# A hybrid recurrence and attention layer on one core: the attention's reciprocal and normalising product move from VectorE to GpSimd

## The chip, the core and the metric

The program runs on one core of a Trainium2 chip. The core has five engines with a queue each: TensorE (PE, with its weight loads shown apart as PEld), VectorE (DVE), ScalarE (ACT), GpSimd (POOL) and SyncE (SP, which issues most transfers). Each engine takes its instructions strictly in the order of its own queue, and an instruction that waits holds up everything behind it. The metric is the device time of one execution in microseconds (us); lower is better.

## The reference, cut to what matters

Two layers run over 256 context tokens and 256 grid tokens, 1024 wide. Each layer projects the tokens to 4096 columns, runs a gated linear recurrence (4 heads) and a neighbourhood attention (8 heads of 64) side by side, projects the two back, and ends in a mixture of 16 experts of which two are used per token. In the second layer only the grid tokens are asked for. The attention's softmax is what the change touches:

```python
s_lat = jnp.where(mask, s_lat + bias.astype(f32), MASK_VALUE)
s_ctx = jnp.einsum('bhrqd,bhkd->bhrqk', grid(q_plain), k_ctx).astype(f32) * scale
p = jax.nn.softmax(jnp.concatenate([s_lat, s_ctx], axis=-1), axis=-1).astype(v.dtype)
...
o = (jnp.einsum('bhrqk,bhrkd->bhrqd', p[..., :n_lat], v_blk)
     + jnp.einsum('bhrqk,bhkd->bhrqd', p[..., n_lat:], v_ctx))
```

## The kernel before, in words

The part of a layer before the output projection is called the front here (`front`, L471). It walks over 16 chunks of 256 projected columns. For each chunk a weight block comes from HBM, ACT makes its rounded high part `wh` (L422), DVE or POOL the remainder `wl` (L423, called a split below), and PE runs three products per pair of tiles (L427 to L429). The table `SPL` says which engine makes which of a chunk's four splits. Only four `wh` and four `wl` buffers exist, one chunk's worth.

As soon as their columns are there, two kinds of other work are put between the chunks: a recurrence head (`hgrn`, L696, whose long chain runs mostly on DVE, with its rms power at L824 on POOL) and a pair of attention heads (`attention`, L868). Four such pairs run in each layer. A pair is a row of units, one for each 128 query tokens and each of the two heads: 8 units in the first layer (four with 256 keys, four with 512), 4 units with 512 keys in the second. That makes 48 units, 16 of 256 columns and 32 of 512.

One unit is a chain over all engines: PE makes the scores `ats` (L881, L882), DVE adds the bias if the keys are grid tokens (L886) and finds the negated row maximum (L888), ACT takes the exponential `ex` and, in a second instruction, delivers its row sum into `sm` (L890), DVE takes the reciprocal of the sum (L891) and multiplies `ex` by it (L892). PE then transposes `ex` by 128 columns at a time into `atp` (L902), ACT copies that out to `pT` (L904), and PE multiplies by the values into `ato` (L913). `units` below are numbered 0 to 47 in the order of time.

Scores and transposes share two PSUM banks (tag "s"), `ex` has three buffers, `sm` four. In the code the scores of unit i+1 stand before the transposes of unit i. The final order on each engine is not the code's: it is set when the program is built, by a scheduler that spreads projection matmuls between the attention's ones. So a changed cost on one engine moves instructions on others too. On POOL the neighbours of a unit's instructions are splits (L423), the clearing of `kl` (L858), the rotary products (L836), the gate products (L647) and the recurrence's K (L713).

Of the kernel before, what the change touches and what calls it, by code (L numbers as in the profile page):

```python
# [13 lines left out]
ALU = mybir.AluOpType  # L14
# [4 lines left out]
P = 128  # L19
# [167 lines left out]
class Emit:  # L187
# [75 lines left out]
    def run(self):  # L263
        tc, nc, A, ctx = self.tc, self.nc, self.A, self.ctx
        pool = lambda *a, **k: ctx.enter_context(tc.tile_pool(*a, **k))
        self.l = 0
        self.cp = pool(name="const", bufs=1)
        self.xp = pool(name="xp", bufs=1)
        self.dp = pool(name="dram", bufs=1, space=DRAM)
        self.mp = pool(name="misc", bufs=1)  # L270
        self.wp = pool(name="wp", bufs=NWP)
        c = lambda shape, name, dt=F32: self.cp.tile(shape, dt, name=name)
        V, G, S = nc.vector, nc.gpsimd, nc.scalar
        self.ct = c([P, NKEEP], "ct")
        self.lb = c([P, 2, 2, 4], "lb")
        self.ln = c([P, 2, 4, KT], "ln")
        self.wr = c([P, KT, NE], "wr")
        self.br = c([P, NE], "br")
        self.bada = c([P, 2, 96], "bada")
        self.ang = c([P, 2, P], "angt")  # L280
        self.ada = [c([P, 48, 2], f"ada{l}") for l in range(2)]
        self.x = [self.xtile(h) for h in range(2)]

        cc = self.mt([P, 512], "lnss", 1)[:, :4 * KT].rearrange("p (i k v) -> p i k v", i=2, v=2)
        q = nc.sync
        q.dma_start(cc[:, 0], A["cT"])
        self.todo = [(l, b, None) for l in range(2) for b in range(24)]
        self.todo[0] = (0, 0, self.wload(A["wada"][0, 0], 2)[:])
        q.dma_start(self.bada[:], A["bada"].rearrange("l p c -> p l c"))
        ne = _C["ident"][1]  # L290
        q.dma_start(self.ct[:, :ne], A["const"][:, :ne])
        S.activation(cc[:, 1], cc[:, 0], AF.Tanh, scale=0.5)
        V.scalar_tensor_tensor(cc[:, 1], cc[:, 1], 1.0, cc[:, 0], op0=ALU.add, op1=ALU.mult)
        self.scw = c([P, KT, 32 + 2 * NADA - 2], "scw")
        G.memset(self.scw[:], 0.0)
        V.tensor_scalar(self.scw[:, :, 2 * NADA - 2:2 * NADA], cc[:, 1], 0.5, None, op0=ALU.mult)

        for o in (8, 32):
            V.tensor_scalar(self.bada[:, :, 2 * o:2 * o + 16], self.bada[:, :, 2 * o:2 * o + 16], 1.0, None, op0=ALU.add)
        for o in (16, 40):  # L300
            V.tensor_scalar(self.bada[:, :, 2 * o:2 * o + 16], self.bada[:, :, 2 * o:2 * o + 16], IA, None, op0=ALU.mult)
        self.ident = self.cst("ident")
        self.tri16 = c([P, P], "tri16", F16)
        self.one16 = c([P, P], "one16", F16)
        self.iota16 = c([P, CAP], "iota16", F16)
        self.ones32, self.e31 = c([P, 32], "ones32"), c([P, 32], "e31")
        self.neghalf = c([P, 8], "neghalf")
        self.ga, self.gna, self.gc = (c([P, 2, 4], n) for n in ("ga", "gna", "gc"))
        self.lt = c([P, 5, 2, 4], "lt")
        self.hD = self.dp.tile([NT, D], F32, name="hD")  # L310
        self.yD = [self.dp.tile([2 * n, D], F32, name=f"yD{i}") for i, n in enumerate((NT, SEQ))]
        self.late = self.open_step = None
        for l in range(2):
            self.l = l
            self.layer(l)
            if self.stop and self.stop.startswith(f"L{l}"):
                return


    def late_constants(self):  # L320
        nc, A, V, G, S = self.nc, self.A, self.nc.vector, self.nc.gpsimd, self.nc.scalar
        q = nc.sync
        ne = _C["ident"][1]
        q.dma_start(self.ct[:, ne:], A["const"][:, ne:NKEEP])
        ints = self.mt([P, 256], "adasb", 4)
        q.dma_start(ints[:, :P + CAP], A["const"][:, NKEEP:NKEEP + P + CAP])
        q.dma_start(self.lb[:], A["lb"])
        q.dma_start(self.ln[:], A["ln"])
        q.dma_start(self.wr[:], A["wr"])
        q.dma_start(self.br[:], A["br"])  # L330
        q.dma_start(self.ang[:], A["ang"].rearrange("l p c -> p l c"))
        for t, i in ((self.ones32, 0), (self.e31, 31)):
            G.memset(t[:], 0.0)
            G.memset(t[:, i:i + 1], 1.0 / D)
        G.memset(self.neghalf[:], -0.5)
        z = self.mt([P, 512], "lnss", 1)
        G.memset(z[:], 0.0)
        self.zero = z[:]

        V.tensor_copy(self.tri16[:], ints[:, :P])  # L340
        G.memset(self.one16[:], 1.0)
        V.tensor_copy(self.iota16[:], ints[:, P:P + CAP])

        lt = self.lt
        l0, l1 = self.lb[:, 0], self.lb[:, 1]
        V.tensor_tensor(lt[:, 0], l0, l1, op=ALU.max)
        V.tensor_tensor(lt[:, 1], l0, lt[:, 0], op=ALU.subtract)
        V.tensor_tensor(lt[:, 2], l1, lt[:, 0], op=ALU.subtract)
        S.activation(lt[:, 1], lt[:, 1], AF.Exp)
        S.activation(lt[:, 2], lt[:, 2], AF.Exp)  # L350
        V.tensor_tensor(lt[:, 3], lt[:, 1], lt[:, 2], op=ALU.add)
        V.reciprocal(lt[:, 3], lt[:, 3])
        V.tensor_tensor(lt[:, 1], lt[:, 1], lt[:, 3], op=ALU.mult)
        V.tensor_tensor(lt[:, 2], lt[:, 2], lt[:, 3], op=ALU.mult)
        V.tensor_tensor(lt[:, 4], lt[:, 1], lt[:, 2], op=ALU.add)
        V.tensor_tensor(lt[:, 4], lt[:, 4], lt[:, 1], op=ALU.subtract)

        V.tensor_scalar(self.ga[:], lt[:, 4], -0.5, 0.5, op0=ALU.mult, op1=ALU.add)
        V.tensor_scalar(self.gna[:], lt[:, 4], 0.5, -0.5, op0=ALU.mult, op1=ALU.add)
        V.tensor_scalar(self.gc[:], lt[:, 4], 0.5, 0.5, op0=ALU.mult, op1=ALU.add)  # L360
# [507 lines left out]
    def attention(self, j, q, k, kl):  # L868
        nc, V, S = self.nc, self.nc.vector, self.nc.scalar
# [5 lines left out]
        def scores(tt, hh):  # L875
            ps = self.pq("s", "ats")
            N = 512 if tt >= 2 else 256
            plain = (slice(N - 256, N), slice(SEQ + 128 * tt - t0, SEQ + 128 * tt - t0 + 128), slice(SEQ, SEQ + CTX))
            rotated = (slice(0, 256), slice(128 * tt - CTX, 128 * tt - CTX + 128), slice(0, SEQ))
            for o, qs, ks in (plain, rotated)[:N // 256]:  # L880
                nc.tensor.matmul(ps[:, o], q[hh][:, qs], k[hh][:, ks], start=True, stop=False, skip_group_check=True)  # L881
                nc.tensor.matmul(ps[:, o], q[hh][:, qs], kl[hh][:, ks], start=False, stop=True, skip_group_check=True)  # L882
            if tt >= 2:
                bt = self.et([P, 256], "bt", NBT)
                S.dma_start(bt[:], self.A["bias"][l, 2 * j + hh, :, tt - 2, :])
                V.tensor_tensor(ps[:, 0:256], ps[:, 0:256], bt[:], op=ALU.add)  # L886
            st = self.mp.tile([P, 4], F32, tag="sm", bufs=4, name="sm")
            V.tensor_reduce(st[:, 0:1], ps[:, :N], axis=AX.X, op=ALU.max, negate=True)  # L888
            e = ex[tt, hh] = self.t2("ex", "e", N)
            S.activation(e[:], ps[:, :N], AF.Exp, bias=st[:, 0:1], accum_out=st[:, 1:2])  # L890
            V.reciprocal(st[:, 2:3], st[:, 1:2])  # L891
            V.tensor_scalar(e[:], e[:], st[:, 2:3], None, op0=ALU.mult)  # L892

        def trans(tt, hh):
            N = 512 if tt >= 2 else 256
# [22 lines left out]
        for i in range(len(units) + 1):  # L918
            if i < len(units):
                scores(*units[i])  # L920
            if i:
                trans(*units[i - 1])
                if units[i - 1][0] % 2 and units[i - 1][1]:
                    values(units[i - 1][0] // 2)
# [839 lines left out]
```

## Time and profile before

| | |
|---|---|
| time before, median of 3 runs | 1307.35 us (1300.77 to 1309.37) |
| the profiled execution | 1303.5 us, of which 1301.7 us from the first to the last instruction (the span) |
| PE busy in the span | 1179.9 us (91%) |
| DVE busy | 591.0 us (45%) |
| ACT busy | 413.6 us (32%) |
| POOL busy | 333.9 us (26%) |
| granted TensorE clock, mean | 0.963 of full speed |

The attention units lie between 168 and 348 us (first layer) and between 876 and 996 us (second). Busy shares over the span hide that: read the stages. A busy PE is an engine with a matmul under way, and matmuls overlap in the records, so that an idle time of PE is the more reliable thing to read. "Idle before" is attributed to the event that ended the wait.

### The profile page before, as it was taken

The page shows a single profiled execution, that of the slowest core. Times are in us where ns is not written, and L with a number is a line of the kernel's source. Part 1 is how long each engine was busy: PE and PEld are TensorE (multiplying, and loading weights), DVE is VectorE, ACT ScalarE, POOL GpSimd, SP SyncE. Part 2 cuts the span into 40 slices and gives each one's busy share as a digit, 9 for nine tenths or more (in the row PEclk, how much of TensorE's full clock was granted, in tenths as well). Part 3 has the DMA queues.
Part 4 walks back from the last instruction along what each step waited for, and adds up shares of the span by engine and source line. Part 5 has one row for each costly group of instructions (what it writes and reads, how often), then busy time and mean ns, then how long its engine had stood idle before and what let it go on. Part 6 is the DMA issues. An engine that isn't in the chain of part 4 may idle for free. (4 is left out here: it accounts for less than half of the span.)

```text
span 1301.7 us, 22530 instructions
## 1 busy us (share of the span) xinstructions
PE 1179.9 (91%) x8821; PEld 731.9 (56%) x8821; DVE 591.0 (45%) x1364; ACT 413.6 (32%) x905; POOL 333.9 (26%) x349
## 2 busy tenths in 40 slices
PE   6989999999898699998997899998888899999984
PEld 4778767668697333333332488976677644333321
DVE  2466654786645414211110764446786434221215
ACT  2233354453544113211111663245436402001011
POOL 2124243322333210111000344254434211112101
PEclk9999999999998699999998899999999989999997
DMA  8794315413275699999997733354235889999994
GB/s 299 251 305 186 145 55 208 142 50 106 90 310 208 262 381 372 392 392 389 408 416 283 271 112 130 130 199 185 105 107 221 369 329 388 390 407 409 423 422 177
DMA packets 67683, 339.30 MB, mean 261 GB/s; under 512 B 10003, under 2 KB 17907, under 8 KB 31856
## 3 DMA queue, kind: packets, MB, share of 16 engines
q1 hardware_dynamic: 54016, 315.73, 62.5%
q0 software_dynamic: 5936, 12.58, 2.9%
q10 hardware_dynamic: 7616, 9.44, 2.3%
q8 instruction: 73, 1.20, 0.4%
q14 instruction: 42, 0.34, 0.1%
HBM read 322.79 MB, written 20.45 MB: 264 GB/s over the span
## 5 line engine op out<-in xcount | busy, mean ns | idle before, releaser
L423 POOL TENSOR_TENSOR wl<-w,wh 128x512 fp32r<-128x512 f32 x121 | 167.0, 1396 | 184.8 <-ACT wh L422 167.1
L1364 PE MATMUL pgA<-we,xgT 128*64 128x512 f32 x688 | 164.6, 612 | 2.6 <-DMA we<-in_wgu_dram 2.6
L427 PE MATMUL pscm<-xh,wh 128*128 128x512 f32 (+1 forms) x320 | 118.2, 374 | 3.5 <-ACT wh L422 2.3
L428 PE MATMUL pscm<-xl,wh 128*128 128x512 f32 (+1 forms) x320 | 119.9, 377 | 0.3 <-DVE xl L423 0.2
L429 PE MATMUL pscm<-xh,wl 128*128 128x512 f32 (+1 forms) x320 | 117.4, 370 | 1.4 <-POOL wl L423 1.4
L422 ACT ACTIVATE wh<-w 128x512 fp32r<-128x512 f32 x160 | 96.6, 626 | 50.6 <-PE pscm L428 17.4
L1364 PEld LDWEIGHTS pgA<-we,xgT 128*64 128x64 f32 x688 | 48.2, 140 | 94.5 <-issue 84.5
L428 PE MATMUL pstm<-wl,xh 128*128 128x256 f32 x320 | 92.4, 289 | 4.5 <-DVE wl L423 3.2
L429 PE MATMUL pstm<-wh,xl 128*128 128x256 f32 x320 | 91.4, 286 | 0.0
L427 PE MATMUL pstm<-wh,xh 128*128 128x256 f32 x320 | 91.0, 285 | 0.0
L1428 POOL DMA_INDIRECT yD<-y,ss x25 | 23.1, 922 | 236.5 <-DVE y L1416 81.6
L1401 PE MATMUL pdA<-we,hdT 128*64 128x512 f32 x320 | 76.4, 611 | 3.3 <-DMA we<-in_wd_dram 3.2
L1364 PE MATMUL pgA<-mw,xgT 128*64 128x512 f32 x336 | 77.7, 598 | 0.0
L1355 DVE COPY xgT<-ptx 128x256 f32<-128x256 f32 (+1 forms) x32 | 15.4, 482 | 135.6 <-PE ptx L1349 90.9
L427 PEld LDWEIGHTS pscm<-xh,wh 128*128 128x128 f32 x320 | 60.6, 191 | 14.3 <-ACT wh L422 2.4
L428 PEld LDWEIGHTS pscm<-xl,wh 128*128 128x128 f32 x320 | 61.3, 192 | 10.5 <-DVE xl L423 0.9
L429 PEld LDWEIGHTS pscm<-xh,wl 128*128 128x128 f32 x320 | 60.8, 191 | 10.7 <-POOL wl L423 2.1
L1382 DVE SCALAR_TENSOR_TENSOR hid<-hid,pgA 128x256 f32<-128x256 f32 x32 | 13.5, 421 | 114.1 <-ACT hid L1381 113.9
L428 PEld LDWEIGHTS pstm<-wl,xh 128*128 128x128 f32 x320 | 61.0, 191 | 6.7 <-DVE wl L423 3.6
L1381 ACT ACTIVATE hid<-pgA 128x256 f32<-128x256 f32 x32 | 12.3, 384 | 160.6 <-PE pgA L1364 160.6
L429 PEld LDWEIGHTS pstm<-wh,xl 128*128 128x128 f32 x320 | 61.1, 191 | 1.0 <-issue 0.8
L427 PEld LDWEIGHTS pstm<-wh,xh 128*128 128x128 f32 x320 | 61.0, 191 | 0.5
(383 smaller groups left out, 2327.3 us busy)
## 6 DMA issues: line engine op xcount, KB each, us to landing
we<-in_wgu_dram SPq DMA_DIRECT2D x86, 1024.0 KB, 14.0
mw<-in_wgu_dram SPq DMA_DIRECT2D x42, 1024.0 KB, 11.1
w<-in_wada_dram SPq DMA_DIRECT2D x41, 1024.0 KB, 7.0
we<-in_wd_dram SPq DMA_DIRECT2D x40, 1024.0 KB, 16.1
w<-in_win_dram SPq DMA_DIRECT2D x29, 1024.0 KB, 5.4
mw<-in_wd_dram SPq DMA_DIRECT2D x24, 1024.0 KB, 16.2
w<-in_wout_dram SPq DMA_DIRECT2D x11, 1024.0 KB, 4.9
wa<-in_wada_dram SPq DMA_DIRECT2D x6, 1024.0 KB, 9.3
```

The source lines that it names most:

```text
L422: self.nc.scalar.activation(hi, src, AF.Copy)
L423: leng.tensor_tensor(lo, src, hi.bitcast(F32), op=ALU.subtract)
L427: mm(out, lh, rh, start=first, stop=False, **k)
L428: mm(out, lh, rl, start=False, stop=False, **k)
L429: mm(out, ll, rh, start=False, stop=last, **k)
L1355: V.tensor_copy(t[:, 0:4, :c], src)
L1364: mm(pA[64 * j:64 * j + 64, :], xgT[e][:, k, 0:64], wk[:, 512 * j:512 * j + 512], start=(k == 0), stop=(k == KT - 1), skip_group_check=Tru ...
L1381: S.activation(h, ps[:, :n], AF.Tanh, scale=0.5)
L1382: V.scalar_tensor_tensor(h, h, 1.0, ps[:, :n], op0=ALU.add, op1=ALU.mult)
L1401: mm(dA[64 * j:64 * j + 64, :], hdT[e][:, kb, 0:64], wk[:, 512 * j:512 * j + 512], start=(kb == 0), stop=(kb == 3), skip_group_check=True, ...
L1428: G.indirect_dma_start(out=self.yD[l][:], out_offset=bass.IndirectOffsetOnAxis(ap=idx, axis=0), in_=y[:c], in_offset=None, bounds_check=2 ...
```

## The change

Two instructions of each unit go from DVE's queue to POOL's. POOL is not given a reciprocal; it raises the sum to the power -1 with a constant tile of -1.0, made once. The product keeps its form, with a scalar for each partition.

```diff
         self.neghalf = c([P, 8], "neghalf")
+        self.negone = c([P, 8], "negone")
...
         G.memset(self.neghalf[:], -0.5)
+        G.memset(self.negone[:], -1.0)
...
             S.activation(e[:], ps[:, :N], AF.Exp, bias=st[:, 0:1], accum_out=st[:, 1:2])
-            V.reciprocal(st[:, 2:3], st[:, 1:2])
-            V.tensor_scalar(e[:], e[:], st[:, 2:3], None, op0=ALU.mult)
+            G = self.nc.gpsimd
+            G.tensor_tensor(st[:, 2:3], st[:, 1:2], self.negone[:, 0:1], op=ALU.pow)
+            G.tensor_scalar(e[:], e[:], st[:, 2:3], None, op0=ALU.mult)
```

In the changed kernel the power is line 894 and the product line 895; lines of the attention behind them stand three further on (the transposes are L905), earlier ones two (the splits are L425).

On POOL, at the start of the first attention pair of the first layer (`wl` are the splits, `kl` the cleared key parts, `K2` the recurrence's K), before:

```order
L423 TENSOR_TENSOR wl_0_1752<-w8_21_1741,wh_0_1751 128x512
L423 TENSOR_TENSOR wl_0_1756<-w8_21_1741,wh_0_1755 128x512
L858 MEMSET kl0_0_1927 64x512
L713 TENSOR_SCALAR K2_0_2332<-uff_1784 128x512
L423 TENSOR_TENSOR wl_0_1844<-w8_24_1841,wh_0_1843 128x512
L423 TENSOR_TENSOR wl_0_1848<-w8_24_1841,wh_0_1847 128x512
L858 MEMSET kl1_0_1928 64x512
```

and in the change:

```order
L425 TENSOR_TENSOR wl_0_1754<-w8_21_1743,wh_0_1753 128x512
L425 TENSOR_TENSOR wl_0_1758<-w8_21_1743,wh_0_1757 128x512
L894 TENSOR_TENSOR sm_1598<-sm_1598,negone_102 128x1
L895 TENSOR_SCALAR ex_1600<-ex_1600,sm_1598 128x256
L894 TENSOR_TENSOR sm_1607<-sm_1607,negone_102 128x1
L895 TENSOR_SCALAR ex_1609<-ex_1609,sm_1607 128x256
```

The first unit's power stands behind all four splits of the chunk that PE is about to use; on POOL nothing stood there before.

On POOL, in the second half of the same pair (units 5 to 7), before:

```order
L858 MEMSET kl0_0_1927 64x512
L713 TENSOR_SCALAR K2_0_2332<-uff_1784 128x512
L423 TENSOR_TENSOR wl_0_1844<-w8_24_1841,wh_0_1843 128x512
L423 TENSOR_TENSOR wl_0_1848<-w8_24_1841,wh_0_1847 128x512
L858 MEMSET kl1_0_1928 64x512
L423 TENSOR_TENSOR wl_0_1852<-w8_24_1841,wh_0_1851 128x512
```

and in the change:

```order
L894 TENSOR_TENSOR sm_1675<-sm_1675,negone_102 128x1
L860 MEMSET kl0_0_1929 64x512
L895 TENSOR_SCALAR ex_1677<-ex_1677,sm_1675 128x512
L715 TENSOR_SCALAR K2_0_2334<-uff_1786 128x512
L425 TENSOR_TENSOR wl_0_1846<-w8_24_1843,wh_0_1845 128x512
L894 TENSOR_TENSOR sm_1696<-sm_1696,negone_102 128x1
L895 TENSOR_SCALAR ex_1698<-ex_1698,sm_1696 128x512
L860 MEMSET kl1_0_1930 64x512
L425 TENSOR_TENSOR wl_0_1850<-w8_24_1843,wh_0_1849 128x512
L894 TENSOR_TENSOR sm_1716<-sm_1716,negone_102 128x1
L895 TENSOR_SCALAR ex_1718<-ex_1718,sm_1716 128x512
L425 TENSOR_TENSOR wl_0_1854<-w8_24_1843,wh_0_1853 128x512
```

Each of the last two units now has one split ahead of its power, and the last splits of the next chunk stand behind the units' powers and products.

On PE, units 2 and 3 of that pair (`ats` scores, `atp` transposes, `pscm` projection), before:

```order
L881 MATMUL ats_1629<-ks1_0_1425,qs1_0_1384 128x256
L882 MATMUL ats_1629<-kl1_0_1427,qs1_0_1384 128x256
L428 MATMUL pscm_1759<-xl4_0_130,wh_0_1751 128x512
L902 MATMUL atp_1638<-ct_69,ex_1621 128x128 x2
L429 MATMUL pscm_1759<-xh4_0_122,wl_0_1752 128x512
L427 MATMUL pscm_1759<-xh5_0_123,wh_0_1751 128x512
L428 MATMUL pscm_1759<-xl5_0_131,wh_0_1751 128x512
L881 MATMUL ats_1642<-ks0_0_1424,qs0_0_1383 128x256
```

and in the change:

```order
L883 MATMUL ats_1631<-ks1_0_1427,qs1_0_1386 128x256
L884 MATMUL ats_1631<-kl1_0_1429,qs1_0_1386 128x256
L905 MATMUL atp_1640<-ct_69,ex_1623 128x128 x2
L430 MATMUL pscm_1761<-xl4_0_131,wh_0_1753 128x512
L431 MATMUL pscm_1761<-xh4_0_123,wl_0_1754 128x512
L429 MATMUL pscm_1761<-xh5_0_124,wh_0_1753 128x512
L883 MATMUL ats_1644<-ks0_0_1426,qs0_0_1385 128x256
```

One projection matmul that stood ahead of the transposes now stands behind them.

## Rows read from the trace of the kernel before

**Rows 1.** The page: busy us and share of the span, each engine.
```profile
PE 1179.9 (91%) x8821; PEld 731.9 (56%) x8821; DVE 591.0 (45%) x1364; ACT 413.6 (32%) x905; POOL 333.9 (26%) x349
```

**Rows 2.** Windows around attention pairs: length, busy by engine, clock, DMA; sum over eight.
```profile
165.00:190.00 25.00, 22.32 (x126) 16.28 (x124) 14.56 (x30) 13.68 (x34) 10.82 (x10) 1.00 0.20 64
875.00:891.00 16.00, 10.94 (x64) 8.41 (x62) 15.59 (x35) 10.05 (x24) 8.29 (x8) 1.00 0.57 221
...
sum 159.00, PE 141.40 PEld 108.56 DVE 111.50 ACT 92.97 POOL 51.31; mean PE 17.67 PEld 13.57 DVE 13.94 ACT 11.62 POOL 6.41
```

**Rows 3.** Line 902, the transposes: what ended PE's waits, us and times.
```profile
  DVE ex L892: 9.6, 11
  DVE sm L891: 2.7, 2
```

**Rows 4.** PE's other waits, 150 to 400 and 740 to 1010: total us, times, longest.
```profile
PE hgt L662 <- DVE ah L659: 3.2, 2, 1.7
...
PE hgX L776 <- DVE K L797: 4.0, 2, 2.9
```

**Rows 5.** DVE by line and form: busy us, mean ns, idle before.
```profile
L892 DVE TENSOR_SCALAR ex<-ex,sm 128x512 f32<-128x512 f32 x32 | 17.1, 535 | 0.7
...
L891 DVE RECIPROCAL sm<-sm 128x1 f32<-128x1 f32 x48 | 7.6, 158 | 12.8 <-ACT ex L890 12.7
L892 DVE TENSOR_SCALAR ex<-ex,sm 128x256 f32<-128x256 f32 x16 | 6.8, 428 | 0.4
```

**Rows 6.** Single lines: shortest, median, longest ns, first and last start, form.
```profile
L892 DVE TENSOR_SCALAR ex<-ex,sm x48: 342/479/1491, 169.2 to 994.1; 128x512 f32<-128x512 f32 x32, 128x256 f32<-128x256 f32 x16
L1660 POOL TENSOR_TENSOR lnst<-lnst,neghalf x2: 577/1048/1520, 1291.9 to 1294.0; 128x1 f32<-128x1 f32 x2
L1078 POOL TENSOR_TENSOR lnst<-lnst,neghalf x5: 697/702/726, 389.7 to 1031.5; 128x2 f32<-128x2 f32 x5
L713 POOL TENSOR_SCALAR K<-uff x4: 621/693/802, 63.9 to 220.4; 128x512 f32<-128x512 f32 x4
```

**Rows 7.** Timeline of unit 0: start us, us, instruction, idle before.
```profile
167.24 3.83 POOL L423 TENSOR_TENSOR wl<-w,wh 128x512 fp32r<-128x512 f32 x3
168.34 0.39 PE L427 MATMUL pscm<-xh,wh 128*128 128x512 f32 x1
168.57 0.40 PE L428 MATMUL pscm<-xl,wh 128*128 128x512 f32 x1
168.75 0.20 ACT L890 ACTIVATION_READ_ACCUMULATOR ex<-ats,sm 128x1 f32 x1
168.99 0.16 DVE L891 RECIPROCAL sm<-sm 128x1 f32<-128x1 f32 x1 [0.62 <-ACT ex L890]
169.18 0.75 DVE L892 TENSOR_SCALAR ex<-ex,sm 128x256 f32<-128x256 f32 x1
170.08 0.41 PE L902 MATMUL atp<-ct,ex 128*128 128x128 f32 x2 [0.41 <-DVE sm L891]
```

**Rows 8.** Timeline of unit 6.
```profile
182.30 0.19 ACT L890 ACTIVATION_READ_ACCUMULATOR ex<-ats,sm 128x1 f32 x1
...
183.53 1.84 DVE L712 TENSOR_SCALAR F<-F 128x512 f32<-128x512 f32 x1
185.47 0.49 DVE L892 TENSOR_SCALAR ex<-ex,sm 128x512 f32<-128x512 f32 x1
186.10 0.63 PE L902 MATMUL atp<-ct,ex 128*128 128x128 f32 x4 [2.10 <-DVE ex L892]
```

**Rows 9.** Timeline of unit 45.
```profile
987.73 0.19 ACT L890 ACTIVATION_READ_ACCUMULATOR ex<-ats,sm 128x1 f32 x1
989.17 0.65 PE L902 MATMUL atp<-ct,ex 128*128 128x128 f32 x4
```

**Rows 10.** Timeline near the end: the longer power of line 1660, and DVE beside it.
```profile
1294.03 1.52 POOL L1660 TENSOR_TENSOR lnst<-lnst,neghalf 128x1 f32<-128x1 f32 x1 [1.60 <-DVE lnst L1659]
...
1293.86 1.27 DVE L1662 SCALAR_TENSOR_TENSOR zt<-zt,lnst,ln 128x1024 f32<-128x1024 f32 x1
```

## The prediction, made before the change was run

> **What bounds the kernel now.** The page's first part gives PE 91% of the span and POOL 26% [rows 1]. That invites the thought that POOL has room for anything, but an average over 1302 us says nothing about the stretches where the attention runs, so I read windows next. Around the eight attention pairs (159 us together) PE is busy 141.4 us, DVE 111.5 and POOL 51.3 [rows 2]. PE still sets the pace there, and it idles 17.6 us. One of these windows is different: from 875 to 891 us DVE is busy 15.59 of 16.00 us and PE only 10.94. There DVE sets the pace.
>
> Then the wait itself. PE waits 9.6 us for the product and 2.7 us more, 13 times in all, at the transposes [rows 3]. These 12.3 us are the most that a faster product chain could give back at this place. Elsewhere PE's largest waits on DVE are in the recurrence, 4.0 and 3.2 us [rows 4]. So nothing near the whole busy time of the two moved instructions is to be had, and what counts is the length of one chain: from the row sum (end of the accumulator read) to the first transpose.
>
> **The price of one unit.** On an unhindered DVE a unit takes 0.04 us to start, 0.16 for the reciprocal, 0.04 for the step between them and then the product, 0.34 for 256 columns or 0.48 for 512 [rows 6, 7]: 0.58 or 0.72 us. On POOL I price it so. The power: the trace has the same operation for one column twice, at 0.58 and 1.52 us, and for two columns five times, close to 0.70 [rows 6]. I take 0.70, the row that repeats; the ends of the range are 0.58 and the mean of the first two, 1.05. The product: POOL's one-input form of 512 columns takes 0.62 at best and 0.69 in the middle [rows 6]; I take 0.68. For 256 columns no row exists; between half of that (0.34) and all of it (0.68), I take 0.42, nearer to half. Starting costs 0.04 as on DVE, and for the step between the two, 0.06, an estimate. That makes 1.22 us for 256 columns and 1.48 for 512, against 0.58 and 0.72. Every unit's chain is twice as long if both engines are free.
>
> **Where it lies on the path.** DVE was often not free. Unit 0 shows the cheap case: sum at 168.95, transposes at 170.08, because the product ran 0.75 us beside splits on POOL [rows 7]. The new chain would let PE start at 168.95 + 1.22 + 0.15 = 170.32, 0.24 later (0.15 us is what passes in every unit between a product's end and its transposes). Unit 6 shows the other: its sum is there at 182.49, but DVE is inside a 1.84 us instruction of the recurrence, the product ends at 185.96 and PE has waited 2.10 us [rows 8]. POOL would be ready for PE at 184.12, 1.98 earlier. Done so for all 48 units, one after the other in the timeline, 27 come later by 10.2 us together (the first is unit 0, the last unit 45, which goes from 989.17 to 989.55 [rows 7, 9]), and 21 come earlier or had slack; counting of those only what PE's waits hold, they give 7.8 us. Net: +2.4 us.
>
> **POOL's queue.** The order of the change puts unit 0's power behind all four splits. The last of them ends at 171.07 [rows 7], 2.1 us after the sum, so unit 0 starts its power there and PE its transposes at 172.40 (with 0.70 + 0.06 + 0.42 + 0.15) instead of 170.32: +2.1 us more. In later units too a split stands ahead of a power, as at the second place shown above; at three of the 48 (units 14, 15 and 44) POOL reaches that split late. Half a split of 3.83/3 = 1.28 us each: +1.9 us. The splits that now stand behind powers come later by one to three microseconds; PE waited for almost none of them before, and I price this at 1 us, between nothing and three.
>
> **Moved matmuls.** The scheduler puts transposes ahead of one projection matmul in about ten units, as shown for unit 2. Matmuls start 0.23 us apart [rows 7]. Where PE then waits for POOL anyway, that filler has lost its use: 10 times 0.23, half of it counted, +1.1 us.
>
> **What DVE gives back.** 7.6 + 17.1 + 6.8 = 31.5 us of DVE's busy time go [rows 5]. DVE is not the pace in seven of eight windows, so most of that hides beside PE. It helps where PE waits for the recurrence: of the 7.2 us [rows 4] I count 40%, -3 us. The one memset that makes the constant stands in an early stretch where POOL idles: nothing. Exponentials, copies and values stay as they are, and no transfer is added. On SP's queue one expert block of the second layer moves behind ten others of its kind; the same bytes go in the same stretch, so I cost it nothing, at worst the few us of one block. What the fronts lose or win reaches the end of the kernel: behind each front PE has the same work, and in the second layer the expert loads on SP's queue wait for buffers that the last attention pair frees.
>
> **The sum:** 2.4 + 2.1 + 1.9 + 1.0 + 1.1 - 3.0 = +5.5 us, against the profiled execution of 1303.5 us: 1309.0. That execution lies 3.85 us below the median of the runs, 1307.35, so for the median I predict 1307.35 + 5.5 = 1312.9, rounded to **1313 us**. A change of 1%, 13 us, is about what a measurement of this kernel tells from none; this is within it.
>
> **Rival 1, slower: POOL's power costs what its worse row says.** The 1.52 us power at 1294.03 began while a DVE instruction with two SBUF inputs (1.27 us from 1293.86) was running and ended after it; the 0.58 us one did not have that [rows 6, 10]. In the attention windows DVE is busy 111.5 of 159 us [rows 2], much of it with such instructions, so many powers could meet one. Place: all 48 units. At 1.05 us on average the same reading of the timeline gives 35 units that come later by 20.8 us and waits given back of only 5.2: +15.6 in place of +2.4. In the first pair POOL's 10.82 busy us of 25 [rows 2] would become 10.82 + 8 x 1.05 + 4 x 0.42 + 4 x 0.68 = 23.6, so its queue would be the pace there. It decides from a mean of about 0.9 us upwards. Time: 1307.35 + 5.5 + 13.2 = 1326. Against it: the five two-column powers hardly vary. Chance 0.22.
>
> The Trainium skill (SBUF — State Buffer, "Who interferes with whom") says that GpSimd and VectorE share a pair of SBUF ports as an exclusive lock, and that a VectorE instruction with two SBUF inputs excludes a GpSimd one that reads SBUF, whichever began second waiting for the whole of the other. By that rule 1.05 or more would be the price wherever the recurrence runs beside a unit, and the time 1326. The trace agrees with the rule in the one case of 1.52 us, and the 0.75 us product beside splits is the same from the other side; how often a power meets such an instruction no row shows.
>
> **Rival 2, faster: the waits on DVE vanish.** If most of the longer chains are covered by projection matmuls, what remains is that DVE no longer stands in PE's way: the 12.3 us at the transposes [rows 3] and half of the 7.2 in the recurrence [rows 4] go, and of the 10.2 us of later starts half is hidden. 1307.35 - 12.3 - 3.6 + 5.1 = 1297. For it speaks the window from 875 us, where DVE is full. Against it: the scheduler put the transposes nearer to the scores, not farther, so cover was taken away. Chance 0.12, half of it past 1%.
>
> **Chances and range.** My forecast, 1304 to 1320, has 0.66; rival 1 has 0.22, rival 2 0.12. Faster by over 1% (below 1294.3): half of rival 2, 0.06. Slower by over 1% (above 1320.4): rival 1, 0.22. The rest, 0.72, is within 1%. The range runs from 1299, which cuts off the better part of rival 2, to 1329, which takes in rival 1 with the upper price of the power.
>
> **What the changed profile would show.** The power (L894) near 0.7 us and the product (L895) near 0.42 and 0.68: the price holds; a mean power of 0.9 or more is rival 1. PE's wait at the transposes (L905), now on POOL, between 14 and 20 us where 12.3 were; under 8 is rival 2. In the window of the second layer's first pair (around 875 us) DVE should have 2 to 3 us less and PE idle less; in the first pair PE should wait some 2 us more at the first transposes, behind the splits. POOL's busy time should grow by 48 x 0.70 + 32 x 0.68 + 16 x 0.42 = 62 us, DVE's fall by 31. I would be wrong if the new order moved something outside the fronts: the expert part behind each front should keep its length.

## The result, and the profile after

| | before | after |
|---|---|---|
| median of the runs, us | 1304.06 (1297.36 to 1309.37) | 1350.67 (1348.54 to 1356.37) |
| the profiled execution: time, span, us | 1303.5, 1301.7 | 1352.3, 1350.4 |
| PE busy / not busy in the span, us | 1179.9 / 121.8 | 1194.5 / 155.9 |
| granted clock, mean | 0.963 | 0.952 |

The change makes the kernel slower: 1.0359 times the time of before, 95% interval 1.0331 to 1.0387. That is 47 us where 5.5 were forecast, and it lies above the whole range (1299 to 1329).

First the page's busy line of the changed kernel, which answers [rows 1].

```profile
PE 1194.5 (88%) x8821; PEld 740.6 (55%) x8821; DVE 564.6 (42%) x1268; ACT 414.4 (31%) x905; POOL 425.9 (32%) x446
```

DVE lost 26.4 us, as the 31.5 of [rows 5] said roughly. POOL gained 92 us where 62 were forecast: the moved instructions cost more than they were priced at. PE runs the same 8821 matmuls and is busy 14.6 us longer, since it had the lower clock for more of the time. The other 34.1 of the span's 48.7 us are idle time of PE. Nearly all of the loss lies where the attention runs: from the first row sum to the last transposes the first layer takes 32.0 us longer (210.9 for 179.0) and the second 14.1 (132.3 for 118.2).

The second view takes POOL's instructions by line and form (busy us, mean ns, idle before), as [rows 5] did for DVE:

```profile
L895 POOL TENSOR_SCALAR ex<-ex,sm 128x512 f32<-128x512 f32 x32 | 51.5, 1609 | 3.1
L894 POOL TENSOR_TENSOR sm<-sm,negone 128x1 f32<-128x1 f32 x48 | 27.9, 581 | 41.6 <-ACT ex L892 41.3
...
L895 POOL TENSOR_SCALAR ex<-ex,sm 128x256 f32<-128x256 f32 x16 | 15.5, 970 | 1.6
```

The power (L894) is cheaper than the 0.70 us forecast. The product (L895) takes 1.61 and 0.97 us, over twice the 0.68 and 0.42 of the forecast. The single lines (shortest, median, longest ns), to hold against [rows 6]:

```profile
L894 POOL TENSOR_TENSOR sm<-sm,negone x48: 537/567/1017, 167.9 to 1038.3; 128x1 f32<-128x1 f32 x48
...
L895 POOL TENSOR_SCALAR ex<-ex,sm x48: 925/1569/2064, 168.5 to 1039.2; 128x512 f32<-128x512 f32 x32, 128x256 f32<-128x256 f32 x16
```

The median power lies 0.03 us above the shortest one, so at most a few had to wait for something else (the mean is 0.58). The slow product is no tail either: its median is at 1.57.

The page's row for the transposes shows what PE paid (busy us, mean ns, idle before):

```profile
L905 PE MATMUL atp<-ct,ex 128*128 128x128 f32 x160 | 30.7, 311 | 49.0 <-POOL ex L895 48.8
```

49.0 us of waiting stand where the two lines of [rows 3] made 12.3. The waits of PE in the two attention parts, first 150 to 420 us, then 770 to 1060 (total us, times, longest):

```profile
PE atp L905 <- POOL ex L895: 31.6, 25, 3.8
...
PE hgt L664 <- DVE ah L661: 1.4, 1, 1.4
...
PE atp L905 <- POOL ex L895: 17.1, 11, 4.5
PE hgX L778 <- DVE K L799: 4.0, 2, 2.9
...
PE hgt L664 <- DVE ah L661: 0.9, 1, 0.9
```

PE's waits for `ah`, 3.2 us in the first part [rows 4], are down to 1.4, and in the second from 2.6 to 0.9; the wait for `K` is the 4.0 us it was. So DVE's relief is worth 3.5 us here, and no more.

The timeline of unit 0, to hold against [rows 7] (start us, us, instruction, idle before):

```profile
164.14 3.75 POOL L425 TENSOR_TENSOR wl<-w,wh 128x512 fp32r<-128x512 f32 x3
...
165.66 0.20 ACT L892 ACTIVATION_READ_ACCUMULATOR ex<-ats,sm 128x1 f32 x1
...
167.87 0.55 POOL L894 TENSOR_TENSOR sm<-sm,negone 128x1 f32<-128x1 f32 x1
...
168.51 0.94 POOL L895 TENSOR_SCALAR ex<-ex,sm 128x256 f32<-128x256 f32 x1
169.42 0.56 POOL L894 TENSOR_TENSOR sm<-sm,negone 128x1 f32<-128x1 f32 x1
...
169.50 0.69 PE L905 MATMUL atp<-ct,ex 128*128 128x128 f32 x2 [2.96 <-POOL ex L895]
...
170.42 0.63 PE L431 MATMUL pscm<-xh,wl 128*128 128x512 f32 x1
```

The sum is there at 165.86. The power stands behind the splits until 167.87, the product runs to 169.45, and PE has waited 2.96 us. Then a second cost is to be seen: the two transposes take 0.69 us where they took 0.41 [rows 7], and a projection matmul 0.63 instead of 0.39. From 169.2 to 172.6 us the records have the granted clock at half (1.2 instead of 2.4 GHz), after PE had stood idle.

I take one measure from the records of single instructions for all that follows: the time from the row sum (end of the accumulator read) to the end of the product, summed over the 48 units, called **the chains**. Before they make 62.6 us: 19.5 until the reciprocal starts, 7.6 of it, 11.5 until the product starts and 24.0 of that. After they make 136.2 us: 33.6, 27.9, 7.7 and 67.0.

### The profile page after: what moved, and what is told of

The parts are those of the page before. It is cut to its first block, busy times and chain, and to the rows that moved or that the text cites. A ratio compares the mean times of both kernels' runs of the same rounds, so it can differ in the third digit from the quotient of the medians.

```text
span 1350.4 us, 22562 instructions
## 1 busy us (share of the span) xinstructions
PE 1194.5 (88%) x8821; PEld 740.6 (55%) x8821; DVE 564.6 (42%) x1268; ACT 414.4 (31%) x905; POOL 425.9 (32%) x446
## 5 line engine op out<-in xcount | busy, mean ns | idle before, releaser
L425 POOL TENSOR_TENSOR wl<-w,wh 128x512 fp32r<-128x512 f32 x121 | 165.8, 1386 | 168.9 <-ACT wh L424 141.3
L905 PE MATMUL atp<-ct,ex 128*128 128x128 f32 x160 | 30.7, 311 | 49.0 <-POOL ex L895 48.8
L895 POOL TENSOR_SCALAR ex<-ex,sm 128x512 f32<-128x512 f32 (+1 forms) x48 | 67.0, 1396 | 4.7
L1384 ACT ACTIVATE hid<-pgA 128x256 f32<-128x256 f32 x32 | 12.3, 383 | 162.8 <-PE pgA L1367 162.8
## 6 DMA issues: line engine op xcount, KB each, us to landing
we<-in_wgu_dram SPq DMA_DIRECT2D x86, 1024.0 KB, 15.8
mw<-in_wd_dram SPq DMA_DIRECT2D x24, 1024.0 KB, 17.3
wa<-in_wada_dram SPq DMA_DIRECT2D x6, 1024.0 KB, 12.3
```

What stands on the lines that cost most here:

```text
L425: leng.tensor_tensor(lo, src, hi.bitcast(F32), op=ALU.subtract)
L895: G.tensor_scalar(e[:], e[:], st[:, 2:3], None, op0=ALU.mult)
L905: nc.tensor.transpose(pt[:, 128 * n:128 * n + 128], ex[tt, hh][:, 128 * n:128 * n + 128], self.ident)
L1384: S.activation(h, ps[:, :n], AF.Tanh, scale=0.5)
```

## The experiments

All ratios are to the kernel before, run on the same chip. The theories were: **price** (the two instructions are longer on POOL than forecast), **queue** (POOL gets to them late), **clock** (PE's lower clock makes the loss by itself), and rival 1 of the prediction (the power waits for DVE).

### One of the two instructions alone

The product alone on POOL, the reciprocal on DVE:

```diff
             V.reciprocal(st[:, 2:3], st[:, 1:2])
-            V.tensor_scalar(e[:], e[:], st[:, 2:3], None, op0=ALU.mult)
+            G.tensor_scalar(e[:], e[:], st[:, 2:3], None, op0=ALU.mult)
```

> Reciprocal on DVE again, only the product on POOL. Theory (the product's own duration on POOL, 1.57 us for 512 columns and 0.93 for 256, is what the time went to): the chain from sum to product end is 0.04 + 0.16 + 0.1 + 1.57 = 1.9 us instead of 2.3, so about 0.4 us x 48 units of at most half exposed are given back: 10 us below the change, ratio to before about 1.027. Rival (POOL's queue with the power in it, two instructions per unit, is what costs): half or more of the loss goes, ratio about 1.015. Rival (the new order of matmuls is what costs): the ratio follows the order, not the chain, anywhere from 1.00 to 1.036.

Measured: 1333.01 us, 1.0212 (1.0194 to 1.0230), PE's wait at the transposes 33.2 us.

The power alone on POOL, the product on DVE:

```diff
-            V.reciprocal(st[:, 2:3], st[:, 1:2])
+            G.tensor_tensor(st[:, 2:3], st[:, 1:2], self.negone[:, 0:1], op=ALU.pow)
             V.tensor_scalar(e[:], e[:], st[:, 2:3], None, op0=ALU.mult)
```

> Power on POOL, product back on DVE. Theory (product's duration): the power at 0.57 us and two hand-offs make the chain about 1.3 us against 0.72, so the loss is small, ratio 1.005 to 1.010; PE's waits at the transposes near 20 us. Rival (the queue on POOL): about half the loss stays, ratio 1.018. Rival (order): not tied to the chain.

Measured: 1320.69 us, 1.0122 (1.0105 to 1.0139), wait 24.0 us. The powers of this kernel (L894) and the products of the one before it (L895), as single lines:

```profile
L894 POOL TENSOR_TENSOR sm<-sm,negone x48: 541/551/1022, 170.3 to 1007.6; 128x1 f32<-128x1 f32 x48
```

```profile
L895 POOL TENSOR_SCALAR ex<-ex,sm x48: 913/1562/2063, 170.3 to 1020.2; 128x512 f32<-128x512 f32 x32, 128x256 f32<-128x256 f32 x16
```

The product's part is the larger, and the two add up to 3.3% of the 3.6. Both times lie between the values that price (1.027; 1.005 to 1.010) and queue (1.015; 1.018) had given, so these two runs do not decide between them. The power is at 0.55 us again, 0.60 in the mean: rival 1's mean of 0.9 is not there, although its sign was right.

### Why the product is slow: the form of the instruction

The row that I had priced it by, K of the recurrence (L713) [rows 6], has two operations in the code (`op0=mult, op1=add`), the product only one. The changed kernel with a second step that does nothing to the value:

```diff
-            G.tensor_scalar(e[:], e[:], st[:, 2:3], None, op0=ALU.mult)
+            G.tensor_scalar(e[:], e[:], st[:, 2:3], 1.0, op0=ALU.mult, op1=ALU.mult)
```

> The change, but the product is written with a second step, times 1.0, in the same instruction. Orders on all engines are those of the change. Theory (the one-step form with a scalar per partition is what is slow on POOL, since the recurrence's two-step form of the same size takes 0.62 to 0.77 us): the product takes about 0.77 us, the chain 1.5 us, and the time is what I had forecast, about 8 us over before, ratio 1.006. Rival (writing in place, or reading a scalar that POOL has only just written, is what is slow): the product stays at 1.57 us and the ratio at 1.036. Rival (order of the matmuls): the product gets faster and the ratio stays at 1.03 or above.

Measured: 1329.73 us, 1.0184 (1.0158 to 1.0210). The instructions stand in the same order on every engine as in the changed kernel. Its product:

```profile
L895 POOL TENSOR_SCALAR ex<-ex,sm x48: 479/694/1189, 173.7 to 1016.0; 128x512 f32<-128x512 f32 x32, 128x256 f32<-128x256 f32 x16
```

It takes 0.69 instead of 1.57 us, and 21 of the 47 us are gone: nearly half of the loss was this one form. The rest, 24 us, I had forecast at 8, so a second step of the prediction had failed too.

The forms by themselves, on POOL, behind the kernel's last output (three of each; here four of the eleven lines of the edit):

```diff
+            G.tensor_scalar(fa, fa, fs[:, 0:1], None, op0=ALU.mult)
...
+            G.tensor_scalar(fa, fa, 1.0, None, op0=ALU.mult)
+            G.tensor_scalar(fa, fa, fs[:, 0:1], 1.0, op0=ALU.mult, op1=ALU.mult)
...
+            G.tensor_tensor(fa, fa, fs[:, 0:1].to_broadcast([P, 512]), op=ALU.mult)
```

> The kernel before, and behind its last output 33 POOL instructions on an idle chip: 11 forms, three times each. The time is some 35 us longer for that alone. Theory (form): one-step with a scalar per partition 1.57 us in place and out of place; two-step forms 0.6 to 0.8 in place and out of place. Rival (in place): in place slow, out of place 0.6 to 0.8, whatever the steps. Rival (scalar just written): all of them 0.6 to 0.8, since the scalar here is a constant. One column's power 0.55 us.

Measured, by line (shortest, median, longest ns): one step by a scalar for each partition, in place (L1668) and into another tile (L1669), one step by an immediate (L1670), two steps (L1671), two steps by immediates (L1674), a product of two tensors (L1675), and for 256 columns one step and two steps (L1676, L1677):

```profile
L1668 POOL TENSOR_SCALAR sq<-sq,neghalf x3: 1562/1562/2044, 1294.0 to 1316.6; 128x512 f32<-128x512 f32 x3
L1669 POOL TENSOR_SCALAR sq<-sq,neghalf x3: 1562/1562/1565, 1296.7 to 1318.2; 128x512 f32<-128x512 f32 x3
L1670 POOL TENSOR_SCALAR sq<-sq x3: 1487/1488/1582, 1298.3 to 1319.9; 128x512 f32<-128x512 f32 x3
L1671 POOL TENSOR_SCALAR sq<-sq,neghalf x3: 691/692/693, 1300.0 to 1321.5; 128x512 f32<-128x512 f32 x3
...
L1674 POOL TENSOR_SCALAR sq<-sq x3: 617/617/618, 1302.4 to 1323.9; 128x512 f32<-128x512 f32 x3
L1675 POOL TENSOR_TENSOR sq<-sq,neghalf x3: 1039/1041/1041, 1303.1 to 1324.6; 128x512 f32<-128x512 f32 x3
L1676 POOL TENSOR_SCALAR sq<-sq,neghalf x3: 922/922/923, 1304.3 to 1325.7; 128x256 f32<-128x256 f32 x3
L1677 POOL TENSOR_SCALAR sq<-sq,neghalf x3: 477/477/478, 1305.3 to 1326.8; 128x256 f32<-128x256 f32 x3
```

With nothing beside them the one-step forms of 512 columns take 2.3 times as long as the two-step one by a scalar for each partition and 2.4 times by an immediate; for 256 columns it is 1.9. Writing in place makes no difference, and the scalar here is a constant, so both rivals of that expectation fall. The slow product is a matter of its form, not of DVE's work beside it. The 0.48 us of 256 columns also bear out my halving roughly (0.42). The Trainium skill (GPSIMD Engine Reference, 4.1 "Engine selection") calls elementwise work with one input on GpSimd roughly line-rate; the runs disagree for the one-step form (1.57 us against DVE's 0.48 [rows 6]), and find the two-step one at 0.69.

The fourth corner, the reciprocal on DVE and the two-step product on POOL:

```diff
             V.reciprocal(st[:, 2:3], st[:, 1:2])
-            V.tensor_scalar(e[:], e[:], st[:, 2:3], None, op0=ALU.mult)
+            G.tensor_scalar(e[:], e[:], st[:, 2:3], 1.0, op0=ALU.mult, op1=ALU.mult)
```

> Reciprocal on DVE, product on POOL in two steps (times the scalar, times 1.0). Orders as in the kernel with the product alone on POOL. The chain is 0.04 + 0.16 + 0.1 + 0.69 + 0.05 = 1.0 us, between before (0.72) and the power alone on POOL (1.4). Theory (time follows the chain's length, each tenth of a us over 48 units costs 3 to 4 us with the clock's part): ratio 1.006 to 1.012. Rival (the hand-over to POOL and its queue cost something fixed, whatever the product takes): ratio 1.018, as with the power and the fast product on POOL.

Measured: 1312.24 us, 1.0053 (1.0033 to 1.0074), wait 14.4 us. With power alone 1.0122 and both 1.0184, the prices add: 0.5% for moving the product, 1.2 to 1.3% for the power, and 1.6 to 1.75% for the product's slow form. The last comes from two pairs of versions in which every engine has the same order.

### Cover for the chain

Five transposes of no use were put ahead of each unit's own, so that PE works where it would wait:

```diff
+            for _ in range(5):
+                nc.tensor.transpose(pt[:, 0:128], self.ident, self.ident)
```

> The change, with five transposes of the identity ahead of each unit's own transposes, into the same PSUM bank, where the unit's own overwrite them. They need no product, so PE can work while it waits. They are 240 matmuls of about 0.12 us: 29 us of work that nobody needs, against 49 us of waits. Theory (PE's waits make the clock fall, and half-speed stretches in the fronts, 41 us in the change against 10 before, are a third of the loss): half-speed stretches in the fronts fall to 15 us or less, the waits at the transposes by 20 to 29 us, and the kernel gets faster than the change by 5 to 12 us, ratio to before about 1.030. Rival (only the waits count, the clock is a side effect): same as the change or slower by the fillers that do not fit into waits, ratio 1.036 to 1.045.

Measured: 1378.6 us, 1.0567 (1.0532 to 1.0603). PE was busy 1221.4 us, 26.9 more than in the changed kernel, for 240 more matmuls, and still waited 40.2 us at the fillers and transposes. That lies above both ranges. Inside the attention stretches the records have 17.1 us of half speed, where the change has 37.5 and the kernel before 3.4; yet the filling hardly took the waits' place, it was added to them, so this run is inconclusive on what the clock costs.

Then real cover: the transposes stand two units behind the scores, in the changed kernel and in the one before.

```diff
-        for i in range(len(units) + 1):
+        for i in range(len(units) + 2):
...
-            if i:
-                trans(*units[i - 1])
+            if i > 1:
+                trans(*units[i - 2])
...
```

> The change, with the transposes of a unit two units behind its scores in the code, not one. Theory (the chain has outgrown the time that the order leaves between scores and transposes): waits at the transposes fall from 49 us to 25 or less and the ratio to about 1.018. Rival (POOL itself is the pace in the pairs, eight units of 2.3 us each beside splits): the waits move but stay near 45 us, ratio 1.03 or more.

> The kernel before, with the transposes two units behind the scores in the code. Theory (12 us of waits at the transposes before come from the same short distance): they fall below 6 us and the kernel is 5 to 8 us faster than before, ratio 0.995. Rival (before, the waits come from DVE being inside the recurrence's instructions, not from the distance): no change, 1.000 within 0.003.

Measured: the changed kernel 1334.88 us, 1.0249 (1.0212 to 1.0285), wait 26.3 instead of 49.0 us; the kernel before 1299.28 us, 0.9964 (0.9949 to 0.9978), wait 4.3 instead of 12.5. The second is what its theory gave, the first lies between theory and rival. The cover takes away half of the changed kernel's waits; even so the change costs 2.85% there.

The same cover for the two milder versions, first the product alone in two steps, then power and two-step product:

> The kernel before with two edits: the transposes stand two units behind the scores (alone measured at 0.9964), and the product goes to POOL in its two-step form (alone 1.0053), the reciprocal stays on DVE. If the price of the hand-over to POOL lies in PE's wait at the transposes alone, the second unit of cover hides it: 0.994 to 0.997, with DVE's relief of some 2 us left over, and PE idle at the transposes under 6 us. If a part of the price lies elsewhere (POOL's queue, PE's clock), the two effects add: about 0.9964 x 1.0053 = 1.0017, range 1.000 to 1.004. I expect the second, at 0.6.

> The changed kernel with the product in its two-step form (1.0184), and the transposes two units behind the scores (0.9964 on the kernel before; on the changed kernel from 1.0359 to 1.0249). If the cover hides what the chain on POOL costs: about 1.000 to 1.004. If the late starts of POOL (22 us summed over the units) outlast the cover, the part that stays is like that of the changed kernel, where two thirds stayed: 1.010 to 1.014. I expect the second, at 0.6; PE idle at the transposes 8 to 16 us.

Measured: 1312.98 us, 1.0060 (1.0039 to 1.0080), and 1313.25 us, 1.0063 (1.0039 to 1.0086). Neither lies where a theory had put it: the first is slower than both gave, the second between the two. Against the kernel before with the same cover, the first is 12.5 us longer, though PE waits only 8.9 us at the transposes, 4.6 more. PE is busy 7.5 us longer in the profiled executions (1186.0 against 1178.5), at a clock of 0.956 against 0.962. A part of that is which execution was profiled: that of the kernel before with cover is the fastest of its ten, 4.7 us below their median. Why the clock is lower at all is open.

### Emptying POOL's queue

In the version with power and two-step product, POOL starts the power 26.0 us late, summed over the units, of which I had counted 6. The timeline of unit 24 shows how (its sum is there at 338.54):

```profile
337.79 1.03 POOL L826 TENSOR_TENSOR rms<-rms,neghalf 128x4 f32<-128x4 f32 x1 [4.34 <-DVE rms L825]
...
338.32 0.22 ACT L892 ACTIVATION_READ_ACCUMULATOR ex<-ats,sm 128x1 f32 x1
...
338.79 1.28 POOL L425 TENSOR_TENSOR wl<-w,wh 128x512 fp32r<-128x512 f32 x1
...
340.02 1.41 POOL L649 TENSOR_TENSOR gs<-gth,angt 128x256 f32<-128x256 f32 x2
...
341.38 0.54 POOL L894 TENSOR_TENSOR sm<-sm,negone 128x1 f32<-128x1 f32 x1
...
342.02 0.55 POOL L895 TENSOR_SCALAR ex<-ex,sm 128x256 f32<-128x256 f32 x1
...
342.62 0.69 PE L905 MATMUL atp<-ct,ex 128*128 128x128 f32 x2 [3.32 <-POOL ex L895]
```

The recurrence's power, a split and two gate products stand ahead. So in the next runs all splits of the fronts go to DVE (95 of the 121 `wl` of the form with 512 columns), once as a control in the kernel before, once with power and two-step product, and once in the changed kernel as it is.

```diff
-            eng = SPL[l].get(cnk)
+            eng = "VVVV"
```

> The control for the next: the kernel before, all splits of the projection's chunks on DVE. DVE's busy time grows by about 121 x 0.69 = 84 us and POOL's falls by about 121 x 1.39 = 168 us. DVE then stands more often ahead of the reciprocal, so slower than before: 1.005 to 1.02.

> The changed kernel with the product in its two-step form, all splits of the projection's chunks on DVE: POOL's queue then holds few things beside the powers and products. To be held against the control with the same splits. If what was undersized in the prediction is POOL's queue (22 us of late starts summed over the units, most of them behind splits), the late starts fall to under 10 us and the ratio to the control is far under 1.0184: 0.995 to 1.008. If it is the longer chain itself or something else, the ratio to the control stays at 1.014 to 1.020 although the splits are gone. A reading to keep apart from the first: DVE, now fuller, gains more from giving the two instructions away; that would show as longer waits at the transposes in the control (over 20 us). I expect the first, at 0.6.

> The changed kernel, one-step product and all, with every split of the projection's chunks on DVE. Held against the control with the same splits (1275.16 us, 0.9767). If the price is the chain's length: the product's 67 us against 21 in the control and the power's 28 to 30 against 8, with POOL's late starts down from 34 to about 20, lengthen the 48 chains by some 70 us; at 0.66 to 0.85 of that, +46 to +60 us: ratio to the control 1.036 to 1.047, to the kernel before 1.012 to 1.023. If half of the changed kernel's loss is the queue of splits and the clock that goes with it, the ratio to the control falls to 1.015 to 1.028. I expect the first, at 0.65.

Measured: the control 1275.16 us, 0.9767 (0.9741 to 0.9793); with power and two-step product 1300.81, 0.9968 (0.9949 to 0.9987); the changed kernel with this edit 1324.87, 1.0158 (1.0131 to 1.0186). Against the control that is 1.020 (1.016 to 1.025, from the ends of the two intervals) and 1.040 (1.035 to 1.046). The prices of 1.8% and 3.6% stay, with all the splits out of POOL's queue. The control was expected to be slower than before and is faster: DVE's busy time grew by 21.5 us where 84 were expected, with 95 splits added for the 121 that were counted. With all durations added up, DVE's splits take 67 us more, but its instructions other than splits, reciprocals and products take 541 us where they took 576. So splits on POOL had lengthened them. The price of the second was expected to all but go, and stayed. The third came out as expected. The busy lines of the control and of the second:

```profile
PE 1177.4 (92%) x8821; PEld 731.8 (57%) x8821; DVE 612.5 (48%) x1459; ACT 413.2 (32%) x905; POOL 204.2 (16%) x254
```

```profile
PE 1177.5 (91%) x8821; PEld 728.9 (56%) x8821; DVE 590.1 (45%) x1363; ACT 414.0 (32%) x905; POOL 270.3 (21%) x351
```

PE is busy for the same time in both, to 0.1 us, and so had the same clock (0.962 and 0.963). The spans, 1273.2 and 1298.8, differ by 25.6 us of pure idle time: the clock is no necessary part of the loss. PE's waits in the second, 150 to 410 us, then 720 to 1060:

```profile
PE atp L905 <- POOL ex L895: 17.0, 21, 2.2
...
PE atp L905 <- POOL ex L895: 7.3, 8, 1.6
```

With 0.4 us of smaller waits that is 24.7 us at the transposes; in the control it is 5.5. The late starts did fall (26.0 to 15.1 us), but they are no longer than DVE's in the control (15.8). What the second's chains have more than the control's is the length of the two instructions themselves: 30.0 us of powers for 7.6 of reciprocals, and 34.9 of products for 21.4, less 5.1 between the two. So against the control the queue is not the price here.

The control with the later transposes, the best single edits together:

> The kernel before with two edits: all splits on DVE (alone 0.9767) and the transposes two units behind the scores (alone 0.9964). If the later transposes still cover waits: 0.972 to 0.975. If the emptier chain has left nothing to cover (5.5 us of waits at the transposes in the control against 12.5 before): 0.976 to 0.979. I expect the second, at 0.55.

Measured: 1277.92 us, 0.9784 (0.9752 to 0.9816), as expected where nothing is left to cover. So the fastest version is the control, at 2.3% under the kernel before; whether the later transposes change anything there can't be told.

### All of it side by side

| on POOL | chains, us | more than its control | time more, us | share |
|---|---|---|---|---|
| two-step product | 71.7 | 9.1 | 6.9 | 0.76 |
| power | 79.9 | 17.3 | 15.9 | 0.92 |
| power, two-step product | 93.3 | 30.7 | 24.0 | 0.78 |
| one-step product | 111.4 | 48.8 | 27.7 | 0.57 |
| the change | 136.2 | 73.6 | 46.8 | 0.64 |
| power, two-step product, no splits | 87.7 | 30.0 | 25.6 | 0.85 |
| the change, no splits | 125.1 | 67.4 | 51.0 | 0.76 |
| two-step product, later transposes | 79.8 | 17.6 | 12.5 | 0.71 |
| power, two-step product, later transposes | 93.8 | 31.6 | 12.9 | 0.41 |
| the change, later transposes | 145.1 | 82.9 | 37.2 | 0.45 |

Controls: the kernel before (62.6 us), the one without splits on POOL (57.7), the one with later transposes (62.2). The time is the difference of the ratios times 1304.5 us (without splits and two-step product: of the medians). From 0.57 to 0.92 of what the chains grow by comes out as time, whether the queue holds splits or not; with a unit more of cover, two of three cases lie below that range. A single share is rough: the 6.9 us of the first row are 4.3 to 9.7 by the interval of its ratio. What the new order of the matmuls costs by itself no run separates, since every move of an instruction also changed orders; the two pairs with equal orders differ by the product's form alone.

## Why the prediction was wrong

**The price of the product failed.** "The product: POOL's one-input form of 512 columns takes 0.62 at best and 0.69 in the middle; I take 0.68." The row was one of a two-step instruction; the one-step form measures 1.61 and 0.97 on average. In the chains the forecast has 28.5 us (32 x 0.68 + 16 x 0.42), the run 67.0. This is the largest single error, 38.5 us of chain, and 21 us of time by the run that removes it. It also lay outside the bounds I had kept for it: the upper one, 0.68 for 256 columns, was drawn from the same row.

**POOL's queue was undersized.** "Half a split of 3.83/3 = 1.28 us each: +1.9 us." Together with unit 0's 2.1 and the bare starts that made 6 us until the power starts. Measured are 33.6 after, and 26.0 with the two-step product. The 7.8 us that units were to give back rested on this: in the kernel before, 31.0 us of the chains pass ahead of the two instructions on DVE (19.5 and 11.5), the forecast left 8.8 of that, and the change has 41.3. One queue was exchanged for another. Unit 0 itself was right: its power starts 2.0 us late, and PE idles 2.96 us at the first transposes where it was 0.41, a rise of 2.5 for the "some 2 us" forecast. What was wrong was to look only for splits that were late already in the trace of before. Of the 33.6 us, POOL spends 10.7 on splits, where 4.0 were counted, and 11.2 on the product of the unit ahead, which was not counted at all and is 5.0 with the two-step form; gate products, rotary products and the recurrence's power (unit 24) make 5.3. The step between power and product came to 7.7 us where 2.9 were counted: it takes 0.10 us, not 0.06, and `kl` stands in it in three units. With the two-step product and no splits of the fronts 15.1 us of late starts are left.

**The power was priced too high.** 0.70 us was taken, 0.57 measured: 27.9 us instead of 33.6. Rival 1 needed 0.9, and the median lies at the minimum; the rival had the right sign by a mechanism that the runs don't show. On the moved instructions the Trainium skill's rule of the shared ports (SBUF — State Buffer, "Who interferes with whom") shows as a tail at most: with the splits on DVE, which read two inputs, powers and products with two steps together took 64.9 us instead of 60.1. On DVE's own instructions more of it may show: the 35 us that they lost when 95 splits left POOL point the way of the rule, but no run separates the ports from other causes.

**The sum of these** accounts for the miss. By the forecast's prices the chains make 33.6 + 28.5 + 1.9 + 2.9 + 4.0 = 70.9 us, 8.3 above before. Measured are 136.2: product +38.5, late starts +27.7, step between the two +4.8, power -5.7. The forecast's way of reading the 48 units one by one does hold for the milder versions: done again on the trace of before, with each unit's measured chain in place of the forecast one, it gives +22.7 us for power and two-step product (measured 24.0), 14.0 for the power alone (15.9) and 7.9 for the two-step product alone (6.9). For the one-step product it gives too much, 40.0 (27.7), and 62.4 for the change (46.8). So the lengths were wrong in the first place. One reading in it was too strict: 0.15 us between a product's end and its transposes is not "what passes in every unit" but in 28 of the 48; in the others PE came to them later.

**The clock had no term.** PE's busy time rose by 14.6 us with the same matmuls. The half-speed stretches grew from 95.7 to 129.9 us, and all of that lies inside the attention stretches (3.4 to 37.5). By this accounting the clock is 30% of the loss in the change, half of it with the two-step product (13.6 of 26.3 us of span), none in the version with two-step product and no splits, and 9.4 of 49.4 us in the changed kernel without splits. It follows idle time loosely; no run separated it as a cause.

**What held.** DVE's relief was priced at -3 and showed -3.5. The splits that came later, priced at 1 us, cost nothing to be seen: PE waits 1.8 us in all for POOL's splits where it waited 2.6. The expert part keeps its length within 3 us (from the last transposes to the end 306.6 before, 309.6 after). The signs given in advance that failed are POOL's busy time (+92 for +62) and PE's wait (49.0 for 14 to 20). In the second layer's first pair DVE is relieved, by 3.8 us where 2 to 3 were said, but PE does not idle less (5.9 us for 5.1). The windows of the changed kernel at the first pair of each layer, to hold against the two of [rows 2] (length; busy of PE, PEld, DVE, ACT, POOL; clock, DMA share, GB/s):

```profile
162.00:187.00 25.00, 18.83 (x100) 14.28 (x99) 5.92 (x12) 11.31 (x29) 17.43 (x19) 0.93 0.17 58
906.50:922.50 16.00, 10.10 (x48) 8.07 (x47) 11.76 (x23) 8.50 (x20) 10.71 (x11) 0.79 0.50 205
```

In 16 us at the start of that pair PE does 48 matmuls where it did 64, and its clock is at 0.79 where it was full.

## What to carry to other kernels

A price from a row holds for that row's exact form: compare the operations in the code, not only the opcode and the shape, and where no row has the form, let the upper bound be a multiple of the nearest. When an instruction joins another engine's queue, list for each of its occurrences what stands ahead of it in that queue, all kinds and its own predecessors, and add up the whole chain; here, without the later transposes, 0.57 to 0.92 of each microsecond by which the 48 chains grew was paid, although PE was the busiest engine. An engine that is idle three quarters of the time was the wrong place for a short link in that chain. The opposite move, giving DVE POOL's bulk work (the splits, 0.69 us there and 1.30 on POOL), was worth 2.3%.

## What the runs showed of the hardware

- On GpSimd a tensor-scalar instruction with one operation took 1.56 us for 128x512 f32 (by an immediate 1.49), with two operations 0.69, and for 256 columns 0.92 and 0.48, with nothing beside it. Multiplying by a broadcast tensor, 1.04 us, also beat the one-step form.
- A power of one column took 0.55 to 0.57 us in the middle over 48 instances. The mean was 0.58 in the change and 0.62 with splits on DVE and a two-step product, where the longest took 1.47; the 1.52 us of [rows 10] is such a tail.
- Late in PE's idle time of 2.96 us in unit 0 the records have its clock at half, for 3.4 us, and the two transposes that followed took 0.69 instead of 0.41 us. Two versions with 95.8 and 121.3 us of idle time had the same mean clock (0.962 and 0.963), so the sum of idle time did not decide it here.
- Moving 95 splits from POOL to DVE took 26 us of PE's idle time away (121.8 to 95.8). The transposes' waits are 7.0 us of it and those for the recurrence's K at L776 3.8; where the other 15 come from was not taken apart. In the same move DVE's other instructions became 35 us shorter in sum (576 to 541).
